# Second pass of the attention scores on 128 partition rows, the queries' low part written to both halves

## The chip, the cores and the metric

The kernel runs on one core of one Trainium2 chip. The metric is the device time of a run in microseconds; three runs of the kernel before have a median of 2206.68 us. Five engines work side by side, each through its own queue in order: TensorE (PE in the profile, its weight loads as PEld), VectorE (DVE), ScalarE (ACT), GpSimd (POOL) and SyncE (SP), which issues the DMAs.

## The reference, cut to what matters

One step of a layer for a prompt of 1024 tokens and a sample of 64 tokens with a cache of 1024. Four token mixers run over one projection of the input; the change is in mixer B, the forgetting attention with 8 heads of 64:

```python
def fox_attend(q, k, v, cq, ck, q_start):
    tq, tk = q.shape[1], k.shape[1]
    s = jnp.einsum('bqhd,bkhd->bhqk', q, k).astype(F32) * FX_HD ** -0.5
    s = s + jnp.swapaxes(cq, 1, 2)[..., :, None] - jnp.swapaxes(ck, 1, 2)[..., None, :]
    mask = jnp.arange(tk)[None, :] <= (q_start + jnp.arange(tq))[:, None]
    p = jax.nn.softmax(jnp.where(mask, s, NEG_BIG), axis=-1)
    return jnp.einsum('bhqk,bkhd->bqhd', p.astype(v.dtype), v)
```

The results of the four mixers are merged with gates, then follow an output projection with a norm, and a feed-forward part with a second norm.

## The kernel before

Everything is in f32, and the large matmuls are made of fp32r parts: a number is split into a high part (rounded to fp32r) and a low part (the rest, as fp32r), and `mm3` (lines 255 to 257) adds three matmuls for each 128 rows of the contraction: high by high, high by low, low by high. `dense` runs such a projection for 128 output columns of a weight, in three chunks of 384, 384 and 320 tokens. The mixers come in the order D, C, B, A. Within B the heads go in four pairs u = 0 to 3: the generator `P_B(u)` makes keys, queries and values of a pair with `dense`, and `M_B(u)` makes its attention. `branch` and `weave` emit `M_B(u-1)` side by side with `P_B(u)`, and the last `M_B(3)` beside the gates' dense work. So the attention's small matmuls lie between dense ones on TensorE. The framework's scheduler then sets each engine's order by its own estimates; buffers rotate in pools, and semaphores are put in by it.

`P_B` writes, for each head hh of a pair, a tile `kks[hh]` of 128 rows: the head's 64 rows r = 64 hh to 64 hh + 63 hold the keys' high part, the other 64 rows their low part (lines 927 and 928). `M_B` goes over 8 row blocks i of 128 queries. On every second i it makes, for 256 queries, a tile `q1` per head, with the queries' high part on both halves (GpSimd, line 1026), and one tile `ql` for both heads, each head's low part on its own 64 rows (VectorE, line 1027; q32 is the f32 query tile). For a head and row block the scores go into a two-bank PSUM tile `ps`, over Lw = max(128 (i + 1), 256) columns, in one block up to 512 columns and in two equal ones above. A block has two matmuls: a first pass (line 1038), whose 128 rows give high queries by high and by low keys at once, and a second pass (line 1040), low queries by high keys on the head's 64 rows. The last block of a row block adds the causal mask with a bf16 matmul of the identity (line 1043).

Then VectorE takes the scores with their bias and the smallest of them (line 1048), ScalarE the exponent with its sum (1053), VectorE the reciprocal and the scale (1054, 1055). One step later `second` transposes the weights `Pt` on TensorE (line 987) into PSUM, ScalarE and VectorE copy them to `PT` in turns (992, 994), and `third` multiplies with the values (line 1012, 64 output rows a head).

Of the kernel before, what the change touches and what calls it, by code (L numbers as in the profile page):

```python
# [9 lines left out]
F32 = mybir.dt.float32  # L10
F32R = mybir.dt.float32r
# [8 lines left out]
P = 128  # L20
D = 1024
# [47 lines left out]
def trunk_kernel(ctx: ExitStack, tc: tile.TileContext, I, O, dbg=None):  # L69
    nc = tc.nc  # L70
    PE, V, S, G, SP = nc.tensor, nc.vector, nc.scalar, nc.gpsimd, nc.sync
# [30 lines left out]
    def small(shape, s, bufs=3, dt=F32):  # L102
        return temps[1].tile(list(shape), dt, tag=s, name=nm(s), bufs=bufs)
# [4 lines left out]
    def const(shape, s, dt=F32):  # L108
        return cp.tile(list(shape), dt, tag=s, name=s)

    # ------------------------------------------------------------------ constants
    ident = const([P, P], "ident")
    make_identity(nc, ident)
    identb = const([P, P], "identb", BF16)
# [31 lines left out]
    mhalf = const([P, 1], "mhalf")  # L146
    V.memset(mhalf, -0.5)

    # ------------------------------------------------------------------ activations, transposed and split
    xh, xl = {}, {}  # L150

    def xtiles(s):
# [24 lines left out]
    def xsrc(tt):  # L177
        return I["x_prompt"][0, tt * P:(tt + 1) * P, :] if tt < 8 else I["x_sample"][0]

    # ------------------------------------------------------------------ weights: load, split, ring  # L180
    plan = []

    def win(c0):
# [73 lines left out]
            PE.matmul(ps, wl, mh, start=False, stop=i == n - 1)  # L257

    def mm2(ps, pairs):
        """as mm3, with both parts of 64 stationary columns side by side, to be added up by addup"""  # L260
        n = len(pairs)
        for i, (w, mh, ml) in enumerate(pairs):
            PE.matmul(ps, w, mh, start=i == 0, stop=False)
            PE.matmul(ps, w, ml, start=False, stop=i == n - 1)
# [20 lines left out]
            yield from g  # L285

    def weave(a, na, b, nb):
        """emit two streams side by side, na steps of a over nb steps of b"""
        live = [True, True]
        done = [0, 0]  # L290
        while live[0] or live[1]:
            i = 0 if live[0] and (not live[1] or done[0] * nb <= done[1] * na) else 1
            try:
                next((a, b)[i])
                done[i] += 1
            except StopIteration:
                live[i] = False

    # ------------------------------------------------------------------ start
    xtiles("x")  # L300
    pk = const([P, PK1], "pk")
    pkr = slot([P, P], F32, "pkr")
# [33 lines left out]
    n = PK1 - PK_NG  # L336
# [59 lines left out]
    oml = const([P, 4], "oml")  # L396
    V.tensor_scalar(oml, lb, -1.0, 1.0, OP.mult, OP.add)

    # ------------------------------------------------------------------ the sixteen gate columns, as rows
    zr_d = dp.tile([16, T], F32, name="zr_d")  # L400
    ls_d = dp.tile([16, T], F32, name="ls_d")
    cr_d = dp.tile([8, T], F32, name="cr_d")
# [122 lines left out]
            V.tensor_copy(mcol[0:TS, 8, 4 * j:4 * j + 4], p3[0:TS, 8, :])  # L525
            yield

    # ------------------------------------------------------------------ gated merge of one branch
    y_d = [[dp.tile([P, T], F32, name=f"y_d{m}_{j}") for j in range(3)] for m in range(4)]
    ylast = {}  # L530
    tails = []
# [67 lines left out]
        br(6)  # L599
        return res  # L600

    # ------------------------------------------------------------------ D: conv and RG-LRU
    SEG = ((0, TP, 3, 0), (TP, TS, TP + 6, TP + 3))
    wab = {}
    stD = const([P, 8, 4], "stD")
# [108 lines left out]
        SP.dma_start(O["p_rg_conv"][0, 0].rearrange("a (r p) -> (a r) p", p=P), so[8:20, :])  # L714
        SP.dma_start(O["s_rg_conv"][0, 0].rearrange("a (r p) -> (a r) p", p=P), so[20:32, :])

    # ------------------------------------------------------------------ C: HGRN2
    ams = []

    def blk(t, n=34):  # L720
# [31 lines left out]
    def M_C(u):  # L752
# [4 lines left out]
                V.memset(am, 0.0)  # L757
                ams.append(am)
        ou = oml[:, u:u + 1]
        # log of the forget gate: log sigmoid(z) + log(1 + lb exp(-z)), and sigmoid(-z)  # L760
        L = slot(s="L")
        S.activation(L, z, AF.Abs)
        S.activation(L, L, AF.Exp, scale=-1.0)
# [146 lines left out]
            yield  # L910
        tails.extend((lambda: tail(4, 8), lambda: tail(8, 9)))

    # ------------------------------------------------------------------ B: forgetting attention
    qbd = []

    def P_B(u):
        r0, r1 = slice(0, 64), slice(64, 128)
        k32 = slot(s="fk")
        bk = bc(FX_K + u * P)

        def evk(c, n0, n, ps):
            S.activation(k32[:, n0:n0 + n], ps, AF.Identity, bias=bk)
        yield from dense(("in", FX_K + u * P), evk)
        # each head's keys, both parts stacked on the partitions
        kks = [slot(dt=F32R, s="fkk") for _ in range(2)]
        for kk, r, q in zip(kks, (r0, r1), (r1, r0)):
            G.tensor_scalar(kk[r], k32[r], 1.0, 1.0, OP.mult, OP.mult)
            V.tensor_sub(kk[q], k32[r], kk[r].bitcast(F32))
        ks = small([P, TS], "fks", 2)
        G.tensor_copy(ks, k32[:, TP:T])  # L930
        q32 = slot(s="fq")

        def evq(c, n0, n, ps):
            S.activation(q32[:, n0:n0 + n], ps, AF.Identity, bias=bq8[:, u:u + 1], scale=0.125)
        dq = dense(("in", FX_Q + u * P), evq)
        next(dq)
        yield
        ko = slot([P, 9, P], s="fko")
        tok(ko, k32, "k", u)
        yield from dq  # L940
        vT = slot(s="fvT")
        bv = bc(FX_V + u * P)

        def evv(c, n0, n, ps):
            S.activation(vT[:, n0:n0 + n], ps, AF.Identity, bias=bv)
        yield from dense(("in", FX_V + u * P), evv)
        st["B", u] = kks, ks, q32, vT
# [2 lines left out]
        return ap.rearrange("t h d -> t (h d)")[:, u * P:(u + 1) * P]  # L950

    def tok(dst, src, nme, u):
        """keys or values with the tokens on the partitions, as they are returned"""
        for g0, g1 in ((0, 4), (4, 8), (8, 9)):
            w = tw(g0)
            pt = bank("m")
            p3 = pt.rearrange("p (a b) -> p a b", b=P)
            for tt in range(g0, g1):
                PE.transpose(p3[0:w, tt - g0, :], src[:, tt * P:tt * P + w], ident)
            if nme == "v":  # L960
                S.activation(dst[0:w, g0:g1, :], p3[0:w, 0:g1 - g0, :], AF.Copy)
            else:
                V.tensor_copy(dst[0:w, g0:g1, :], p3[0:w, 0:g1 - g0, :])
        SP.dma_start(flat(O["p_fox_" + nme][0, 0], u).rearrange("(t p) c -> p t c", p=P), dst[:, 0:8, :])
        SP.dma_start(flat(O["s_fox_" + nme][0, 0], u), dst[0:TS, 8, :])

    def M_B(u):
# [48 lines left out]
        for i in range(8):  # L1016
            L = (i + 1) * P
            if i % 2 == 0:
                t2 = slice(i * P, i * P + 2 * P)
                q1s = []  # L1020
                ql = small([P, 2 * P], "ql", 2, F32R)
                for hh in range(2):
                    r = slice(64 * hh, 64 * hh + 64)
                    q1 = small([P, 2 * P], f"q1{hh}", 2, F32R)
                    for h in (slice(0, 64), slice(64, 128)):
                        G.tensor_scalar(q1[h], q32[r, t2], 1.0, 1.0, OP.mult, OP.mult)
                    V.tensor_sub(ql[r], q32[r, t2], q1[r].bitcast(F32))
                    q1s.append(q1)
            qi = slice(i % 2 * P, i % 2 * P + P)
            for hh in range(2):  # L1030
                r = slice(64 * hh, 64 * hh + 64)
# [4 lines left out]
                for b in range(nb):  # L1036
                    s0, s1, o0 = b * n, b * n + n, 512 * b
                    PE.matmul(ps[:, o0:o0 + n], q1s[hh][:, qi], kks[hh][:, s0:s1], start=True, stop=False)  # L1038
                    last = s1 == Lw
                    PE.matmul(ps[:, o0:o0 + n], ql[r, qi], kks[hh][r, s0:s1], start=False, stop=not last)  # L1040
                    if last:
                        o = o0 + L - P - s0
                        PE.matmul(ps[:, o:o + P], identb, maskb, start=False, stop=True)
                # minus the scores with their bias, and minus the largest of them
                n = min(n, L)
                mn = small([P, 1], "mn", 4)
                Pt = slot([P, TP], s="Pt")
# [14 lines left out]
        second(*prev)  # L1062
        yield
        third()
        # decode rows: both heads on the partitions
        kr = slot([P, 8, P], s="fkr")
        SP.dma_start(kr, flat(I["cache_fox_k"][0, 0], u).rearrange("(t p) c -> p t c", p=P))
        vc = slot([P, 8, P], s="fvc")
# [45 lines left out]
        yput(1, u, y)  # L1114
        yield

    # ------------------------------------------------------------------ A: mLSTM
    def P_A(u):
        kt = slot(s="mkt")
        bk = bk8[:, u:u + 1]  # L1120
# [40 lines left out]
    def M_A(u):  # L1161
# [27 lines left out]
        yield  # L1189

        def first(c):
            """decays and scores of a block, and its keys with the tokens on the partitions"""
            w, t0 = tw(c), c * P
            pss, wes = [], []
            for hh in range(2):
# [100 lines left out]
            tails.extend((lambda hh=hh: tail(hh, 4, 8), lambda hh=hh: tail(hh, 8, 9)))  # L1296
        yield

    # ------------------------------------------------------------------ the token mixers
    def branch(m, Pg, Mg, n, nP, nM, it, ng=4):  # L1300
        for u in range(1, n):
            weave(Mg(u - 1), nM, Pg(u), nP)
# [24 lines left out]
    branch(0, P_A, M_A, 2, 18, 21, 3)  # L1327
    res = merge(0, 3)

    # ------------------------------------------------------------------ w_out, norm  # L1330
    phase("F")
    xtiles("mix")
    mxh, mxl = dict(xh), dict(xl)
# [72 lines left out]
                if i > 2:  # L1406
                    xsplit(acc[seq[i - 3]], seq[i - 3])

    # ------------------------------------------------------------------ gated conv feed-forward
    stF = const([P, 4, 16], "stF")  # L1410
    hs = {}

# [44 lines left out]
        SP.dma_start(O["y_prompt"][0, tt * P:tt * P + P, :] if tt < 8 else O["y_sample"][0], acc[tt][0:tw(tt)])  # L1457

    def stats(r, ps, al):
        """a tile's mean and its 1 / deviation, in halves"""  # L1460
        bst = small([P, 2, 6], "lst", 2)
        mv = small([P, 2], "lmv", 3)
        for hf, sl in enumerate(hfs):
            pinned(V.tensor_tensor(r[:, sl], r[:, sl], ps[:, sl], OP.add))
            pinned(V.bn_stats(bst[:, hf, :], r[:, sl]))
        pinned(V.bn_aggr(mv, bst))
        rs = small([P, 1], "lrs1", 2)
        pinned(V.tensor_scalar(rs, mv[:, 1:2], 1e-5, None, OP.add))
        G.tensor_tensor(rs, rs, mhalf, OP.pow)
        return mv, rs  # L1470

    def finish(s6, s7, gb, bb):
        """the last two tiles' norm, on the vector engine alone"""
        for tt, (mv, rs) in ((6, s6), (7, s7)):
            r = acc[tt]
            if tt == 7:
# [107 lines left out]
```

## Time and profile before

| | |
|---|---|
| runs, us | 2205.98, 2206.68, 2207.47 (median 2206.68) |
| profiled execution, span from first to last instruction | 2204.7 us |
| median of the runs less that span | 2.0 us |
| TensorE busy | 2161.4 us, 98% |
| VectorE / ScalarE / GpSimd busy | 1065.3 / 563.4 / 392.2 us |
| score matmuls, first to last start | 735.7 to 1043.5 us |
| TensorE clock granted | 1.00 in the stretch of the scores |

The profiled execution's own device time isn't listed apart from its span. In the profile a line such as L1040 is line 1040 of the kernel. A shape `64*128 64x320` means a stationary operand of 64 rows by 128 columns and a moving operand of 64 rows by 320 columns. Ends of matmuls are modelled, and matmuls overlap, so the distance from one start to the next says more than a duration.

### The profile page before, as it was taken

To read this page: it belongs to the slowest core of one execution; us is meant where nothing else is said; L and a number is where in the kernel's file an instruction comes from. 1 tells how busy PE (TensorE), PEld (TensorE's weight loads), DVE (VectorE), ACT (ScalarE), POOL (GpSimd) and SP (SyncE) were. 2 spreads that over 40 slices of the span, in tenths; PEclk is the share of its full clock that TensorE was granted. 3 is DMA by queue.
4 is the path that set the end of the run, shared out by engine and by line. 5 is a ranking of instruction groups with operands and counts; after the bars stand their busy time and mean duration, and the time that the engine had idled before them with its cause. 6 is when DMAs were issued, how large, how long until landed. Compare 5 with 4: busy or idle time off the path is not lost.

```text
span 2204.7 us, 31659 instructions
## 1 busy us (share of the span) xinstructions
PE 2161.4 (98%) x13203; PEld 1989.1 (90%) x13203; DVE 1065.3 (48%) x2020; ACT 563.4 (26%) x1100; POOL 392.2 (18%) x360
## 2 busy tenths in 40 slices
PE   8999999999999999999999999999999999999997
PEld 7999999888899887788999988997899999999996
DVE  4643346667334446445332144545564444444447
ACT  2753034454210333333201122221130011101111
POOL 1111001121123211111131102123320000000014
PEclk9999999999999999999999999999999999999999
DMA  5112321111133232130432112234101111111112
GB/s 148 52 59 89 100 63 39 43 52 44 63 132 127 67 91 78 51 88 26 136 130 78 59 31 82 73 119 159 48 20 43 34 58 39 48 48 39 48 57 83
DMA packets 174763, 156.76 MB, mean 71 GB/s; under 512 B 12637, under 2 KB 155305, under 8 KB 174621
## 3 DMA queue, kind: packets, MB, share of 16 engines
q1 hardware_dynamic: 174620, 154.74, 22.3%
q8 instruction: 104, 1.70, 0.3%
q14 instruction: 39, 0.31, 0.1%
HBM read 124.65 MB, written 30.06 MB: 70 GB/s over the span
## 4 chain that ended last, share of the span: by engine, by line
PE 85%; DVE 6%; issue 6%; POOL 1%; DMA 1%; ACT 0%; SPq 0%; DVEq 0%; POOLq 0%; ACTq 0%
PE psd L255 16%; PE psd L256 15%; PE psd L257 15%; PE psm L255 5%; PE psm L256 5%; PE psm L257 5%; PE pss L255 4%; PE pss L256 4%; PE pss L257 4%; PE psm L987 1%; DVE wl L244 1%; PE psm L1012 1%; PE pss L1040 1%; PE pss L1038 1%; POOL wh L243 1%
## 5 line engine op out<-in xcount | busy, mean ns | idle before, releaser
L255 PE MATMUL psd<-xh,wh 128*128 128x384 f32 (+1 forms) x1920 | 643.4, 335 | 1.0 <-ACT xh L164 0.9
L257 PE MATMUL psd<-xh,wl 128*128 128x384 f32 (+1 forms) x1920 | 631.8, 329 | 0.0
L256 PE MATMUL psd<-xl,wh 128*128 128x384 f32 (+1 forms) x1920 | 630.6, 328 | 0.5 <-DVE xl L165 0.5
L243 POOL TENSOR_SCALAR wh<-wr 128x1024 fp32r<-128x1024 f32 x144 | 155.0, 1078 | 1275.1 <-PE psd L256 436.9
L255 PEld LDWEIGHTS psd<-xh,wh 128*128 128x128 f32 x1920 | 363.2, 189 | 8.0 <-issue 3.0
L256 PEld LDWEIGHTS psd<-xl,wh 128*128 128x128 f32 x1920 | 362.0, 189 | 1.9 <-DVE xl L165 0.9
L257 PEld LDWEIGHTS psd<-xh,wl 128*128 128x128 f32 x1920 | 361.8, 188 | 0.5 <-DVE wl L244 0.2
L244 DVE TENSOR_TENSOR wl<-wr,wh 128x1024 fp32r<-128x1024 f32 x144 | 210.3, 1464 | 253.8 <-POOL wh L243 241.7
L552 ACT ACTIVATE th<-psd,bhalf 128x384 f32<-128x384 f32 (+1 forms) x96 | 53.9, 563 | 340.4 <-PE psd L257 339.7
L255 PE MATMUL psm<-yh,wh 128*128 128x384 f32 (+1 forms) x384 | 126.0, 330 | 7.7 <-DVE th L587 7.7
L255 PE MATMUL psd<-x1h,wh 128*128 128x384 f32 (+1 forms) x384 | 125.5, 327 | 0.7 <-DVE x1l L175 0.7
L255 PE MATMUL psm<-x1h,wh 128*128 128x384 f32 (+1 forms) x384 | 125.3, 326 | 0.7 <-DVE cv L1444 0.7
L256 PE MATMUL psm<-yl,wh 128*128 128x384 f32 (+1 forms) x384 | 125.5, 327 | 0.3 <-DVE yl L572 0.3
L257 PE MATMUL psm<-yh,wl 128*128 128x384 f32 (+1 forms) x384 | 125.7, 327 | 0.0
L257 PE MATMUL psd<-x1h,wl 128*128 128x384 f32 (+1 forms) x384 | 125.3, 326 | 0.0
L257 PE MATMUL psm<-x1h,wl 128*128 128x384 f32 (+1 forms) x384 | 125.2, 326 | 0.0
L256 PE MATMUL psd<-x1l,wh 128*128 128x384 f32 (+1 forms) x384 | 125.2, 326 | 0.0
L256 PE MATMUL psm<-x1l,wh 128*128 128x384 f32 (+1 forms) x384 | 125.2, 326 | 0.0
L587 DVE SCALAR_TENSOR_TENSOR th<-th,psm 128x384 f32<-128x384 f32 (+1 forms) x96 | 50.3, 529 | 107.6 <-PE psm L257 106.4
L1421 ACT ACTIVATE gp<-psd 128x384 f32<-128x384 f32 (+1 forms) x48 | 22.0, 457 | 302.3 <-PE psd L257 302.3
L1497 DVE SCALAR_TENSOR_TENSOR acc<-acc,pss 128x1024 f32<-128x1024 f32 x54 | 65.9, 1221 | 65.4 <-PE pss L257 64.7
L255 PE MATMUL pss<-wh,hh 128*128 128x512 f32 x208 | 83.0, 399 | 0.0
(479 smaller groups left out, 3570.0 us busy)
## 6 DMA issues: line engine op xcount, KB each, us to landing
wr<-in_w_in_dram SPq DMA_DIRECT2D x48, 512.0 KB
wr<-in_w_mg_dram SPq DMA_DIRECT2D x32, 512.0 KB
mx_d<-th SPq DMA_DIRECT2D x24, 544.0 KB
prev<-mx_d SPq DMA_DIRECT2D x24, 544.0 KB
wr<-in_w_br_dram SPq DMA_DIRECT2D x16, 512.0 KB
wr<-in_w_ff_gate_dram SPq DMA_DIRECT2D x16, 512.0 KB
wr<-in_w_ff_up_dram SPq DMA_DIRECT2D x16, 512.0 KB
wr<-in_w_ff_down_dram SPq DMA_DIRECT2D x16, 512.0 KB
```

The costliest lines, as they stand in the source:

```text
L243: G.tensor_scalar(h, raw, 1.0, 1.0, OP.mult, OP.mult)
L244: V.tensor_sub(l, raw, h.bitcast(F32))
L255: PE.matmul(ps, wh, mh, start=i == 0, stop=False)
L256: PE.matmul(ps, wh, ml, start=False, stop=False)
L257: PE.matmul(ps, wl, mh, start=False, stop=i == n - 1)
L552: S.activation(th[:, n0:n0 + n], ps, AF.Tanh, bias=b, scale=0.5)
L587: V.scalar_tensor_tensor(th[:, n0:n0 + n], th[:, n0:n0 + n], 1.0, ps[:, :n], OP.add, OP.mult)
L987: PE.transpose(p3[0:sw, j, 0:w], Pt[:, s0:s0 + sw], ident[0:w, 0:w])
L1012: PE.matmul(po[64 * h:64 * h + 64, 0:P], vt[:, j, 64 * h:64 * h + 64], pair[h][:, j, :], start=j == 0, stop=j == i)
L1038: PE.matmul(ps[:, o0:o0 + n], q1s[hh][:, qi], kks[hh][:, s0:s1], start=True, stop=False)
L1040: PE.matmul(ps[:, o0:o0 + n], ql[r, qi], kks[hh][r, s0:s1], start=False, stop=not last)
L1497: V.scalar_tensor_tensor(acc[tt], acc[tt], al, ps, OP.mult, OP.add)
```

## The change

`ql` is now one tile per head, `qls[hh]`, with the head's low query part on both halves, made by two subtractions in place of one. The second pass takes all 128 rows of `qls[hh]` and of `kks[hh]`; so it also adds the low queries by the low keys. The tiles ql0 and ql1 have two buffers each, as ql had. Comments are taken out elsewhere, and line numbers from 1028 on rise by one or two (1038 is now 1040, 1040 is 1042, 1043 is 1045, 1055 is 1057).

```diff
-                q1s = []
-                ql = small([P, 2 * P], "ql", 2, F32R)
+                q1s, qls = [], []
                 for hh in range(2):
                     r = slice(64 * hh, 64 * hh + 64)
                     q1 = small([P, 2 * P], f"q1{hh}", 2, F32R)
+                    ql = small([P, 2 * P], f"ql{hh}", 2, F32R)
                     for h in (slice(0, 64), slice(64, 128)):
                         G.tensor_scalar(q1[h], q32[r, t2], 1.0, 1.0, OP.mult, OP.mult)
-                    V.tensor_sub(ql[r], q32[r, t2], q1[r].bitcast(F32))
+                    for h in (slice(0, 64), slice(64, 128)):
+                        V.tensor_sub(ql[h], q32[r, t2], q1[r].bitcast(F32))
                     q1s.append(q1)
+                    qls.append(ql)
...
-                    PE.matmul(ps[:, o0:o0 + n], ql[r, qi], kks[hh][r, s0:s1], start=False, stop=not last)
+                    PE.matmul(ps[:, o0:o0 + n], qls[hh][:, qi], kks[hh][:, s0:s1], start=False, stop=not last)
```

TensorE, first pair of heads, end of row block i=1 and start of i=2, before (`fkk` is kks, `q` is q1, the numbers tell buffers apart):

```order
L1038 MATMUL pss_6722<-fkk_6395,q_911_6651 128x256
L1040 MATMUL pss_6722<-fkk_6395,ql_6646 128x256
L1043 LDWEIGHTS identb
L1043 MATMUL pss_6722<-maskb,identb 128x128
L1012 MATMUL psm_6733<-PT_6677,fvt_6594 64x128
L1038 MATMUL pss_6751<-fkk_6394,q_937_6743 128x384
L1040 MATMUL pss_6751<-fkk_6394,ql_6742 128x384
L1012 MATMUL psm_6733<-PT_6718,fvt_6594 64x128
```

The same place on TensorE after the change:

```order
L1040 MATMUL pss_6725<-fkk_6395,q_911_6652 128x256
L1042 MATMUL pss_6725<-fkk_6395,ql_912_6653 128x256
L1045 LDWEIGHTS identb
L1045 MATMUL pss_6725<-maskb,identb 128x128
L1012 MATMUL psm_6736<-PT_6680,fvt_6594 64x128
L1040 MATMUL pss_6757<-fkk_6394,q_937_6745 128x384
L1042 MATMUL pss_6757<-fkk_6394,ql_938_6746 128x384
L1012 MATMUL psm_6736<-PT_6721,fvt_6594 64x128
```

No score matmul has moved; the second pass now reads a ql of its own for each head. Elsewhere on TensorE some transposes (L987) stand one to six dense matmuls earlier or later.

VectorE at the softmax of row block i=1 of the first pair, before (`fq` is q32; sm, Pt and mn belong to the softmax):

```order
L1027 TENSOR_TENSOR ql_6900<-fq_6402,q_975_6901 64x256
L1054 RECIPROCAL sm_6714<-sm_6714 128x1
L1027 TENSOR_TENSOR ql_6900<-fq_6402,q_976_6905 64x256
L1055 TENSOR_SCALAR Pt_6712<-Pt_6712,sm_6714 128x256
L1054 RECIPROCAL sm_6729<-sm_6729 128x1
L1055 TENSOR_SCALAR Pt_6727<-Pt_6727,sm_6729 128x256
L1048 ISA Pt_6756,mn_6755<-pss_6751,fcb_6590 128x384
```

The same place on VectorE after the change:

```order
L1028 TENSOR_TENSOR ql_977_6907<-fq_6402,q_976_6906 64x256
L1056 RECIPROCAL sm_6717<-sm_6717 128x1
L1028 TENSOR_TENSOR ql_977_6907<-fq_6402,q_976_6906 64x256
L1057 TENSOR_SCALAR Pt_6715<-Pt_6715,sm_6717 128x256
L1056 RECIPROCAL sm_6732<-sm_6732 128x1
L1028 TENSOR_TENSOR ql_979_6913<-fq_6402,q_978_6912 64x256
L1057 TENSOR_SCALAR Pt_6730<-Pt_6730,sm_6732 128x256
L1050 ISA Pt_6762,mn_6761<-pss_6757,fcb_6590 128x384
```

The second head's first subtraction now stands between the reciprocal and the scale of the row block's second head, and its other one behind the next score row.

## Rows read from the trace of the kernel before

**Rows 1.** The page, its parts on busy time and on the chain.

```profile
PE 2161.4 (98%) x13203; PEld 1989.1 (90%) x13203; DVE 1065.3 (48%) x2020; ACT 563.4 (26%) x1100; POOL 392.2 (18%) x360
...
PE 85%; DVE 6%; issue 6%; POOL 1%; DMA 1%; ACT 0%; SPq 0%; DVEq 0%; POOLq 0%; ACTq 0%
```

**Rows 2.** Windows: busy PE, PEld, DVE, ACT, POOL; clock; DMA share; GB/s.

```profile
735.00:1070.00 335.00, 333.46 (x2346) 270.08 (x2345) 167.79 (x394) 123.90 (x283) 52.56 (x84) 1.00 0.24 68
```

**Rows 3.** Waits of PE, 735 to 1070 us: total, times, longest.

```profile
PE psm L987 <- DVE Pt L1055: 1.5, 3, 0.5
```

**Rows 4.** Waits of PEld in the same stretch.

```profile
PEld pss L1040 <- issue: 19.0, 89, 0.3
PEld L1043 <- issue: 9.4, 46, 0.2
PEld pss L1038 <- issue: 7.4, 38, 0.2
```

**Rows 5.** Line 1040: count, min/median/max ns, starts, four commonest forms.

```profile
L1040 PE MATMUL pss<-fkk,ql x96: 379/440/503, 736.1 to 1043.5; 64*128 64x384 f32 x24, 64*128 64x512 f32 x24, 64*128 64x256 f32 x16, 64*128 64x320 f32 x16
```

**Rows 6.** Timeline of PE, ends of two full-array runs: start, duration, engine, line.

```profile
746.50 0.31 PE L257 MATMUL psd<-xh,wl 128*128 128x320 f32 x1
...
748.41 0.34 PE L1038 MATMUL pss<-fkk,q 128*128 128x384 f32 x1
...
2149.67 0.39 PE L257 MATMUL pss<-wh,hl 128*128 128x512 f32 x1
...
2152.92 0.39 PE L256 MATMUL pss<-wd,hh 128*128 128x512 f32 x1
```

**Rows 7.** Timeline of PE at a narrow score row and at a wide one.

```profile
735.89 0.28 PE L1038 MATMUL pss<-fkk,q 128*128 128x256 f32 x1
736.10 0.39 PE L1040 MATMUL pss<-fkk,ql 64*128 64x256 f32 x1
736.42 0.23 PE L1043 MATMUL pss<-maskb,identb 128*128 128x128 bf16 x1
...
841.13 0.41 PE L1038 MATMUL pss<-fkk,q 128*128 128x320 f32 x1
841.48 0.41 PE L1040 MATMUL pss<-fkk,ql 64*128 64x320 f32 x1
841.82 0.23 PE L1043 MATMUL pss<-maskb,identb 128*128 128x128 bf16 x1
841.86 0.39 PE L1038 MATMUL pss<-fkk,q 128*128 128x320 f32 x1
```

**Rows 8.** Chain in order of time: start, length; 384, 448, 448 and 512 columns.

```profile
771.60 0.37 PE pss L1040
...
778.83 0.40 PE pss L1040
779.23 0.40 PE pss L1038
...
784.71 0.43 PE pss L1040
```

**Rows 9.** Timeline: a dense matmul, the load beside it, and a second pass's load.

```profile
735.02 0.33 PE L256 MATMUL psd<-xl,wh 128*128 128x384 f32 x1
...
735.02 0.19 PEld L257 LDWEIGHTS psd<-xh,wl 128*128 128x128 f32 x1
...
736.10 0.18 PEld L1040 LDWEIGHTS pss<-fkk,ql 64*128 64x128 f32 x1 [0.19 <-issue]
```

**Rows 10.** VectorE's ql group (busy, mean ns | idle before); timeline of scales and transposes.

```profile
L1027 DVE TENSOR_TENSOR ql<-fq,q 64x256 fp32r<-64x256 f32 x32 | 14.5, 452 | 18.6 <-PE pss L1040 13.5 <-POOL q L1026 4.6
...
745.43 0.35 DVE L1055 TENSOR_SCALAR Pt<-Pt,sm 128x256 f32<-128x256 f32 x1
746.13 0.38 PE L987 MATMUL psm<-ident,Pt 128*128 128x128 f32 x2
...
751.81 1.33 DVE L1055 TENSOR_SCALAR Pt<-Pt,sm 128x384 f32<-128x384 f32 x1
```

## The prediction

> **What bounds the kernel now.** I read the page first: TensorE is busy for 2161 of 2204.7 us and holds 85% of the chain that ended last [rows 1]. The change touches the stage of the forgetting attention only, so I then read the stretch in which its score matmuls lie, 735 to 1070 us. There TensorE is busy for 333.5 of 335 us, VectorE for 167.8 and ScalarE for 123.9, at full granted clock [rows 2], and the whole list of TensorE's waits is three waits of 0.5 us each [rows 3]. A microsecond taken off TensorE in this stretch comes off the end, unless another engine cannot follow.
>
> Busy is not the same as streaming, though. The weight loads (PEld) show where it isn't: before the load of the second pass (L1040) the loader stands idle 89 times, 19.0 us in all, before the mask's load (L1043) 46 times and before that of the first pass (L1038) 38 times, and all of these are put down to issue, not to another engine [rows 4]. The reader is to see the pattern of shapes: L1040 has the form `64*128` while L1038 and L1043 have `128*128` [rows 5, 7].
>
> What it costs is seen from start to start. Matmuls of `128*128` that follow each other start at the pace of their columns: 13 of 320 columns take 748.41 - 746.50 = 1.91 us, 0.147 each, and 14 of 512 columns take 2152.92 - 2149.67 = 3.25 us, 0.232 each [rows 6]. That is 0.456 ns a column on average, so I take 0.117 us for 256 columns, 0.175 for 384 and 0.204 for 448. Around the second pass the pace is another one [rows 7]: with 320 columns, L1038 to L1040 takes 0.35 us, L1040 to L1043 0.34. With 256 columns L1040 takes 0.32 and L1038, which there follows full-array work, 0.21. The chain gives the other widths as pieces of L1040: 0.37 for 384 columns, 0.40 for 448 and 0.43 for 512, and 0.40 for an L1038 of 448 that follows an L1040 [rows 8]. So L1040 takes 0.19 to 0.20 us more than its columns at every width: a constant, not a rate. An L1038 between two second passes has the same excess, and one that comes from full-array work and goes into L1040 has half, 0.21 - 0.117 = 0.093. I read this as follows: each change of array shape lets the matmul ahead run out (about 0.10 us) and then leaves the next load uncovered (about 0.10 us).
>
> **The change part by part.**
>
> *Second pass at 128 rows.* With qls on both halves, L1040 has the shape of its neighbours, and both changes of shape around it go. L1040 occurs 96 times [rows 5]; the kernel's loops give 16 of 256 columns, 16 of 320, 24 of 384, 16 of 448 and 24 of 512. Its excess: 16 x (0.32 - 0.117) = 3.2; 16 x (0.34 - 0.147) = 3.1; 24 x (0.37 - 0.175) = 4.7; 16 x (0.40 - 0.204) = 3.1; 24 x (0.43 - 0.232) = 4.8. Sum 18.9 us. Of the 96, three are followed by the `128*64` matmuls of L1012, which keep their own change of shape, so 0.3 is left: 18.6 us.
>
> *First pass.* 32 of the 96 L1038 open the second block of a wide score row and lie between two second passes. They lose the whole excess, 0.20 each: 6.4 us. The other 64 lose only the running out, about 0.095: 6.1 us. Their uncovered load, where they follow L1012 or a short transpose, stays. Together the sum on TensorE is 18.6 + 6.4 + 6.1 = 31.1 us. None of this is cover for something else, because TensorE sets the pace of the stretch.
>
> *256 columns.* The trace has no run of full-array matmuls that narrow. Their load has 128 columns like the others, and the nearest row shows loads of this size keeping a pace of 0.147 [rows 6]. If that is their floor, 32 matmuls cost up to 0.03 more than I took, 1.0 us; I take 0.5.
>
> *The mask.* L1043 is bf16 and follows L1040 nearly always. That a bf16 load behind a 128-row f32 matmul costs no running out is not shown. The other direction is: L1043 to L1038 takes 0.04 us [rows 7]. So I take 0 and keep 61 x 0.10 = 6.1 us as the far end. On the other side the mask's own load, idle for 0.2 us 46 times [rows 4], may come to lie under the second pass: half of that idle is the running out counted above, the other half, 46 x 0.1 = 4.6 us, mostly runs beside the next load, which stays uncovered behind so short a matmul. I take none of it and keep 3 us as an end of the range.
>
> *Products added.* The second pass now also adds low query times low key. It streams the same columns, and the pace of a 128-row matmul is that of rows 6, so nothing more.
>
> *VectorE.* Each ql subtraction is made twice: 32 more of 64x256, 0.452 us each, 14.5 us by the group's row [rows 10]. The order shows most of them doubled in place, where VectorE waits anyway (167 us are free in the stretch [rows 2]); so most cost nothing. One place is tight: a new subtraction stands between the reciprocal and the scale of score row i=1, hh=1. The scale there starts at 745.43 and takes 0.35, and the transposes that wait for it start at 746.13 [rows 10], a slack of 0.35. With 0.42 to 0.45 more and TensorE arriving some 0.2 earlier there, a wait of about 0.25 comes up, four times (once a head pair): 1.0 us. The far ends are 0 and, if a quarter of the 32 subtractions were exposed in full, 3.6 us. The three present waits stay as they are: the wait at L987 hangs on a score row's end, through VectorE, and moves with it. SBUF tiles, GpSimd's q1 copies and all DMA issues are unchanged in number and order, so they cost nothing. ScalarE, with 124 of 335 us, follows.
>
> The sum: 31.1 - 0.5 - 1.0 = 29.6 us. The profiled execution has a span of 2204.7 us, 2.0 below the median of the runs, and I carry that difference over: 2206.7 - 29.6 = 2177 us.
>
> **A rule that speaks against it.** The trace shows the load of one 128-row matmul running beside the matmul before it, with the same rows in use: the load for L257 and the matmul of L256 both start at 735.02, while the load for L1040 starts only with an idle 0.19 us before it [rows 9]. The Trainium skill, "TensorE: Matmul & The Clock Gate", Part 3, "The mechanism", lists as seen in traces that weight loads overlap matmuls in flight only when the row group differs. By that sentence a full-height second pass would cover no more than the half-height one and the sum would be zero, rival 2 below; row 735.02 disagrees, and the sum above goes by the row.
>
> **The rivals.**
>
> 1. *The mask keeps its run-out* (a change of type costs as a change of shape does). For: L1043's loads are idle 46 times [rows 4]. Against: 0.04 us in the other direction. Gain 29.6 - 6.1 = 23.5, 2183 us.
>
> 2. *The change doesn't do what it says*: the stall belongs to the pair of operands q and ql or to the accumulation in one bank, and a full-height second pass stalls too. For: every stall lies at this pair. Against: the dense matmuls switch operands and accumulate at full pace. Gain about 0, less the 1.0 on VectorE: 2206 to 2208 us.
>
> 3. *VectorE becomes the one that is waited for.* A large part of the 32 subtractions lands between a score row and its transposes: half of them exposed in full are 7.2 us, gain 30.6 - 7.2 = 23, 2183 us; all of them 14.5, 2191 us.
>
> 4. *Slower.* The same place, but the subtractions come under the slowing that the scale shows at 751.81, where 128x384 takes 1.33 us [rows 10]: each of 32 then holds TensorE for 1.33 us, 42.6 us against 30.6 gained, 2219 us. It decides from 30.6 / 32 = 0.96 us on the path per subtraction. The subtractions of now have a mean of 0.452 [rows 10], with the same neighbours on GpSimd, so nearly all of them would have to be slowed and exposed at once: unlikely.
>
> **How the numbers follow.** The forecast, 2177 us, has a chance of 0.78 with its own bounds: 31.1 (nothing lost) gives 2175.6 and the 3 us at the mask 2172.6; the upper end, 3.6 on VectorE and 1.0 at 256 columns, gives 2180. Rival 1 has 0.07, rival 3 0.07, rival 2 0.04, rival 4 0.04. For 8 in 10 the range goes from 2172.5 to 2186, which takes in rival 1 and the half of rival 3. About 0.2% (4.4 us) is what a measurement of this kernel can tell from no change. Faster by more than that: 0.78 + 0.07 + 0.07 = 0.92; within it 0.04; slower 0.04.
>
> **What would show it.** The second pass reads `128*128` and its pieces of the chain shrink to the pace of rows 6, from 0.34 to about 0.15 at 320 columns; the idle before its loads, 19.0 us, goes nearly to zero, and that before the first pass's from 7.4 to the few behind L1012 and the transposes. TensorE's waits in the stretch grow from 1.5 us to 2 to 5, on the scale. VectorE's ql group counts 64 and about 29 us. The rest of the trace shifts by 30 us and keeps its lengths. It would be wrong if the second pass at `128*128` kept a pace above 0.2 us at 320 columns, or if waits for VectorE of tens of microseconds stood in the list.

## The result and the profile after

The changed kernel takes 2183.14 us (median of 4 runs, 2182.15 to 2185.64); its ratio to the kernel before is 0.9894, 95% interval 0.988 to 0.9908. That is 23.5 us less. The prediction of 2177 us had the way right and the time 6 us too low; 2183 lies inside its range. The profiled execution is the longest of the four, with a span of 2183.9 us.

Tables first. The page's busy times and chain, the stretch from the first to the last score matmul (columns as in [rows 2]) and the waits of TensorE in it (as in [rows 3]). Lines from 1028 on have moved: the first pass is L1040 now, the second L1042, the mask L1045, VectorE's score row L1050 and its scale L1057.

```profile
PE 2133.7 (98%) x13203; PEld 1986.1 (91%) x13203; DVE 1079.4 (49%) x2052; ACT 563.4 (26%) x1100; POOL 396.1 (18%) x360
...
PE 82%; DVE 8%; issue 6%; POOL 2%; DMA 1%; ACT 1%; SPq 0%; DVEq 0%; POOLq 0%; ACTq 0%
```

```profile
736.00:1021.00 285.00, 278.91 (x2123) 243.48 (x2121) 169.81 (x404) 115.98 (x265) 54.75 (x83) 1.00 0.24 69
```

```profile
PE pss L1040 <- DVE mn L1050: 3.6, 3, 1.2
PE psm L987 <- DVE Pt L1057: 2.5, 7, 0.4
```

The score stage is about 24 us shorter, and in it VectorE now has two places where TensorE waits for it: 3.6 us at a first pass, which was not there, and 2.5 us at the transposes, where there were 1.5 [rows 3]. All ten of these waits are new; the three of before are gone.

The stalls of shape are gone. The second pass as its line's view shows it (count, min/median/max ns, first and last start, forms), and the waits of PEld in the stage, to be read against [rows 4, 5]:

```profile
L1042 PE MATMUL pss<-fkk,ql x96: 278/338/481, 736.8 to 1020.6; 128*128 128x384 f32 x24, 128*128 128x512 f32 x24, 128*128 128x256 f32 x16, 128*128 128x320 f32 x16
```

```profile
PEld L1045 <- issue: 8.2, 38, 0.3
PEld pss L1040 <- POOL q L1026: 3.9, 3, 1.3
...
PEld pss L1040 <- issue: 1.0, 6, 0.2
```

L1042 has no idle at all before its loads, where there were 19.0 us. On the timeline of PE (start, duration) the narrow row and the first wide rows of the first pair read:

```profile
736.66 0.28 PE L1040 MATMUL pss<-fkk,q 128*128 128x256 f32 x1
736.78 0.28 PE L1042 MATMUL pss<-fkk,ql 128*128 128x256 f32 x1
736.90 0.23 PE L1045 MATMUL pss<-maskb,identb 128*128 128x128 bf16 x1
...
756.75 0.31 PE L1042 MATMUL pss<-fkk,ql 128*128 128x320 f32 x1
756.90 0.31 PE L1040 MATMUL pss<-fkk,q 128*128 128x320 f32 x1
757.05 0.31 PE L1042 MATMUL pss<-fkk,ql 128*128 128x320 f32 x1
757.20 0.23 PE L1045 MATMUL pss<-maskb,identb 128*128 128x128 bf16 x1
758.63 0.39 PE L1040 MATMUL pss<-fkk,q 128*128 128x320 f32 x1 [1.20 <-DVE mn L1050]
```

At 256 columns both passes take 0.12 us from start to start, at 320 columns 0.15: the pace of the columns. The last two rows show what came instead: from the mask at 757.20 to the next first pass at 758.63 there are 1.43 us, where a mask used to be followed after 0.04 [rows 7].

Added up over all starts of the stage, first and second pass together took 68.3 us before and take 38.0 now, 30.3 less: 12.2 at the first pass and 18.1 at the second. From the first to the last score matmul the stage went from 307.6 to 284.0 us, 23.6 less. The difference of 6.7 lies in the masks with what follows them (5.3 us before, 9.6 now, nearly all of it the three gaps of 1.43) and in dense matmuls with a wait behind them (152.4 and 154.5).

### Where VectorE came in

The timelines of DVE and POOL of the changed kernel at the end of row block i=2 and the start of i=3, first pair; a pair's later twin stands 76 us further on, and the third 153:

```profile
751.11 0.41 DVE L1057 TENSOR_SCALAR Pt<-Pt,sm 128x384 f32<-128x384 f32 x1
751.44 2.54 DVE L1028 TENSOR_TENSOR ql<-fq,q 64x256 fp32r<-64x256 f32 x2
754.01 0.16 DVE L1056 RECIPROCAL sm<-sm 128x1 f32<-128x1 f32 x1
...
755.06 2.69 DVE L928 TENSOR_TENSOR fkk<-fk,fkk 64x1088 fp32r<-64x1088 f32 x2
757.78 0.69 DVE L1050 CUSTOM_DVE_ANT_0 Pt<-pss,fcb 128x512 f32<-128x512 f32 x1
758.40 0.08 DVE L1050 DVE_READ_ACCUMULATOR2_ANT mn<- 128x1 f32 x1
758.51 0.86 DVE L1028 TENSOR_TENSOR ql<-fq,q 64x256 fp32r<-64x256 f32 x2
```

```profile
751.34 2.37 POOL L927 TENSOR_SCALAR fkk<-fk 64x1088 fp32r<-64x1088 f32 x2
755.16 2.87 POOL L1026 TENSOR_SCALAR q<-fq 64x256 fp32r<-64x256 f32 x2 [1.44 <-PE pss L1040]
```

Two subtractions take 0.86 us at 758.51, and 2.54 us at 751.44, beside GpSimd's two copies of the next pair's keys (L927). The queue behind them is late by that: the keys' low part (L928) and then the score row i=3, hh=1, whose matmuls had ended by 755.4 and which VectorE takes only at 757.78. That row holds one of the two PSUM tiles (the memory that the score matmuls write to), and the first pass of i=4, hh=1 waits for it. Before the change VectorE took the same row at nearly the same time, 757.66, but there the row's mask, its last matmul, had started only at 757.03 (timelines of DVE and of PE of the kernel before):

```profile
755.02 2.60 DVE L928 TENSOR_TENSOR fkk<-fk,fkk 64x1088 fp32r<-64x1088 f32 x2
757.66 0.69 DVE L1048 CUSTOM_DVE_ANT_0 Pt<-pss,fcb 128x512 f32<-128x512 f32 x1
...
757.03 0.23 PE L1043 MATMUL pss<-maskb,identb 128*128 128x128 bf16 x1
```

So at this place TensorE's saving ran into a VectorE queue that had not become shorter. Before the change the copies of L927 had stood beside the scale at 751.81 [rows 10], which took 1.33 us; now the scale is through in 0.41 us and the subtractions stand there.

VectorE is not the only one that is late at this first pass. Its load also waits for GpSimd's q1 copies (3.9 us in three, in PEld's list above). Two of these copies take 2.87 us at 755.16, beside VectorE's L928, and end at 758.03; two others had taken 1.23 at 750.02. VectorE lets the PSUM tile go last, at 758.48, and so ends the wait; but with VectorE on time, about 0.8 of each gap of 1.43 us would have stood, by an estimate from these rows.

Three of the seven waits at the transposes (1.0 us) follow 2.35 us behind these first passes, for the scale of the row that VectorE took late. The other four (1.4 us), one for each head pair, lie elsewhere, at row block i=6. VectorE and TensorE in the first pair:

```profile
781.78 0.95 DVE L1028 TENSOR_TENSOR ql<-fq,q 64x256 fp32r<-64x256 f32 x2 [0.38 <-POOL q L1026]
...
782.84 1.21 DVE L1050 CUSTOM_DVE_ANT_0 Pt<-pss,fcb 128x1024 f32<-128x1024 f32 x1
...
783.97 0.68 DVE L1057 TENSOR_SCALAR Pt<-Pt,sm 128x896 f32<-128x896 f32 x1
...
784.80 0.63 PE L987 MATMUL psm<-ident,Pt 128*128 128x128 f32 x4 [0.39 <-DVE Pt L1057]
```

Two subtractions stand here ahead of the next score row and of the scale that the transposes need.

### The profile page after: what moved, and what is told of

The parts are those of the page before. It is cut to its first block, busy times and chain, and to the rows that moved or that the text cites. A ratio compares the mean times of both kernels' runs of the same rounds, so it can differ in the third digit from the quotient of the medians.

```text
span 2183.9 us, 31686 instructions
## 1 busy us (share of the span) xinstructions
PE 2133.7 (98%) x13203; PEld 1986.1 (91%) x13203; DVE 1079.4 (49%) x2052; ACT 563.4 (26%) x1100; POOL 396.1 (18%) x360
## 4 chain that ended last, share of the span: by engine, by line
PE 82%; DVE 8%; issue 6%; POOL 2%; DMA 1%; ACT 1%; SPq 0%; DVEq 0%; POOLq 0%; ACTq 0%
PE psd L255 15%; PE psd L257 15%; PE psd L256 15%; PE psm L255 5%; PE psm L256 5%; PE psm L257 5%; PE pss L255 4%; PE pss L256 4%; PE pss L257 4%; DVE wl L244 2%; PE psm L987 1%; PE psm L1012 1%; POOL wh L243 1%; DVE ql L1028 1%; PE psm L1200 1%
## 5 line engine op out<-in xcount | busy, mean ns | idle before, releaser
L244 DVE TENSOR_TENSOR wl<-wr,wh 128x1024 fp32r<-128x1024 f32 x144 | 210.5, 1465 | 253.5 <-POOL wh L243 239.6
L1432 DVE TENSOR_SCALAR cv<-gp,pk 128x1024 f32<-128x1024 f32 (+1 forms) x32 | 21.1, 698 | 126.9 <-ACT gp L1423 126.9
```

Source lines behind the costliest of these rows:

```text
L244: V.tensor_sub(l, raw, h.bitcast(F32))
```

## The experiments

Six kernels; each ratio below is to runs of the kernel before on the same chip.

### The zero half: shape without the added subtractions

```diff
-                    ql = small([P, 2 * P], f"ql{hh}", 2, F32R)
+                    ql = qz[hh][i // 2 % 2]
...
-                    for h in (slice(0, 64), slice(64, 128)):
-                        V.tensor_sub(ql[h], q32[r, t2], q1[r].bitcast(F32))
+                    V.tensor_sub(ql[r], q32[r, t2], q1[r].bitcast(F32))
```

`qz` holds two tiles per head whose other half is set to zero once, at the start of the stage.

> The second pass keeps its 128 rows, but the half of each ql tile that belongs to the other keys part is zero, written once at the start; each ql subtraction is made once, as in the kernel before (32 in all). Shape theory (the whole gain on TensorE comes from the change of shape, and what is missing of it was eaten by the 32 added VectorE subtractions): TensorE's score matmuls keep the starts of the changed kernel, the waits of L1040 for VectorE and GpSimd (3.6 us) and most of those of the transposes are gone, and the time is 2206.6 - 30 = 2176 to 2179 us, 4 to 7 us below the changed kernel. Rival (the missing part has another cause, such as later stages or the mask): the time stays at 2182 to 2184 us.

2178.15 us, ratio 0.9871 (0.9856 to 0.9886): 28.9 us off, 5 more than the change. Its line of the second pass and its only wait of TensorE in the stage:

```profile
L1047 PE MATMUL pss<-fkk,qz x96: 274/338/481, 735.0 to 1013.1; 128*128 128x384 f32 x24, 128*128 128x512 f32 x24, 128*128 128x256 f32 x16, 128*128 128x320 f32 x16
```

```profile
PE pss L1045 <- DVE mn L1055: 0.5, 3, 0.2
```

From first to last second pass the stage takes 278.1 us, against 283.8 with the change and 307.4 before [rows 5]. The two passes together are at 38.0 us, as in the changed kernel. So the shape alone gives the 30 us on TensorE, and the added subtractions took back 5 to 6. As expected. The rival, that later stages or the mask ate the rest, falls: neither was touched. Three subtractions, one at each of the three places, still run beside the copies of the keys, and 0.39 to 0.45 us are left of each gap of 1.43.

### The subtractions alone

```diff
-                    PE.matmul(ps[:, o0:o0 + n], qls[hh][:, qi], kks[hh][:, s0:s1], start=False, stop=not last)
+                    PE.matmul(ps[:, o0:o0 + n], qls[hh][r, qi], kks[hh][r, s0:s1], start=False, stop=not last)
```

> The changed kernel with the second pass put back on the head's own 64 rows; the 32 added subtractions stay. Shape theory: the stalls around the second pass are all back, and with TensorE as slow as before most of the added VectorE work is hidden: 2206 to 2210 us. Rival (the gain came with the new tiles or the new order of the instructions, not with the shape): clearly below 2200 us.

2209.43 us, ratio 1.0008 (1.0 to 1.0017). The waits of PEld are those of [rows 4] again, and TensorE's list those of [rows 3]:

```profile
PEld pss L1042 <- issue: 19.0, 89, 0.3
PEld L1045 <- issue: 9.4, 46, 0.2
PEld pss L1040 <- issue: 7.4, 38, 0.2
```

```profile
PE psm L987 <- DVE Pt L1057: 1.5, 3, 0.5
```

With the second pass at half height, 32 more subtractions cost next to nothing (0.08%, and the interval reaches down to no change). Three of them run beside the copies of L927 here, for up to 1310 ns each (six do in the changed kernel), and TensorE is late enough for VectorE all the same. So the gain came with the shape and not with new tiles or a new order, and the price of the subtractions depends on how fast TensorE is.

### The keys' high part on ScalarE

```diff
-            G.tensor_scalar(kk[r], k32[r], 1.0, 1.0, OP.mult, OP.mult)
+            S.activation(kk[r], k32[r], AF.Copy)
```

> The changed kernel with the keys' high part (line 927) written by ScalarE in place of GpSimd; all 64 subtractions stay. In the changed kernel two subtractions at 751.4 us take 2.54 us beside two GpSimd copies of line 927, against 0.86 elsewhere, and the score row i=4, hh=1 waits 1.2 us three times after it. Theory of contention between VectorE and GpSimd: without line 927 on GpSimd the two take 0.86 again, the three waits go, and the time is 4 to 6 us below the changed kernel, 2177 to 2179 us. Rival (the number of subtractions in the queue is what delays the chain, whoever else runs): the waits stay at 1 us or move, and the time stays within 1.5 us of 2183 us.

2176.41 us, ratio 0.9863 (0.985 to 0.9877). The waits at the first pass are gone, and the same two subtractions on DVE's timeline take a third:

```profile
746.25 0.41 DVE L1057 TENSOR_SCALAR Pt<-Pt,sm 128x384 f32<-128x384 f32 x1
746.58 0.84 DVE L1028 TENSOR_TENSOR ql<-fq,q 64x256 fp32r<-64x256 f32 x2
```

```profile
PE psm L987 <- DVE Pt L1057: 1.4, 4, 0.4
```

All 64 subtractions are there, so their number does not make the wait at the first pass; what stands beside GpSimd's copies does. The edit frees GpSimd's own queue along with VectorE's, so it does not part the two. The four waits that are left are those at i=6: they are the price of added subtractions away from the copies. The time fell a little more than expected.

The second passes start at 731.9 instead of 736.8 us. Most of that is no effect of the edit. VectorE's timelines ahead of the stage, of the changed kernel and then of this one:

```profile
705.98 2.10 DVE L244 TENSOR_TENSOR wl<-wr,wh 128x1024 fp32r<-128x1024 f32 x1 [8.28 <-POOL wh L243]
708.12 3.38 DVE L928 TENSOR_TENSOR fkk<-fk,fkk 64x1088 fp32r<-64x1088 f32 x2
```

```profile
702.74 1.23 DVE L244 TENSOR_TENSOR wl<-wr,wh 128x1024 fp32r<-128x1024 f32 x1 [8.29 <-POOL wh L243]
704.00 2.60 DVE L928 TENSOR_TENSOR fkk<-fk,fkk 64x1088 fp32r<-64x1088 f32 x2
```

L244 stands ahead of the first pair's keys and starts 3.2 us sooner. That difference between the two profiled executions is there near their start already: TensorE's first matmul of L426 stands at 44.6 and at 41.5 us. The keys' low part ends 4.9 us sooner, at 706.60 against 711.50, so the edit brings the start forward by 1.7. The next experiment prices this.

### The same move on the kernel before

Line 927 as above, nothing else changed.

> The kernel before, with nothing but the keys' high part moved from GpSimd to ScalarE: what that move is worth without the change. Theory: the first score row starts some 4 us earlier, the three waits of 0.5 us in the stage go, and the stage is otherwise as long as before: 2201 to 2204 us. If the move is worth as much here as it was on the changed kernel (6 to 7 us), 2200 us, then it repaired nothing that the change had broken.

2204.28 us, ratio 0.9984 (0.9975 to 0.9993), 3.5 us off; 0.3 above the upper end of what was expected. Its second pass:

```profile
L1040 PE MATMUL pss<-fkk,ql x96: 379/440/502, 733.6 to 1038.9; 64*128 64x384 f32 x24, 64*128 64x512 f32 x24, 64*128 64x256 f32 x16, 64*128 64x320 f32 x16
```

From the first to the last second pass the stage takes 305.3 us, 2.1 less than before. On the changed kernel the move was worth 6.7 us in the runs (2183.14 to 2176.41) and 5.2 in the stage (283.8 to 278.6). So about 3 us, in the runs and in the stage alike, are the contention that the change had run into, and the rest would have come without it.

### Both repairs together

> Both repairs together: the zero half (32 subtractions, each made once) and the keys' high part on ScalarE. Theory (the shape gives 30 us, contention at line 927 had eaten some 6 of them, and line 927 off GpSimd also brings the first score row some 4 us forward): the stage from the first to the last second pass has the length of the zero-half run, 278 us, the start is that of the run with the keys on ScalarE, 732 us, and the time is 2173 to 2176 us. Rival (both repairs and the early start are worth the same thing): 2176 to 2178 us, no lower than the keys on ScalarE alone.

The edits are the two shown above. 2174.76 us, ratio 0.9852 (0.9838 to 0.9865): 33.0 us off, the lowest median here, faster than both the kernel before and the changed one.

```profile
L1047 PE MATMUL pss<-fkk,qz x96: 278/338/472, 733.5 to 1010.4; 128*128 128x384 f32 x24, 128*128 128x512 f32 x24, 128*128 128x256 f32 x16, 128*128 128x320 f32 x16
```

The stage takes 276.9 us and has no wait of TensorE left in it. It starts at 733.5, not at the 732 expected, which had counted in a difference between profiled executions that the keys' move does not make. Against the keys' move alone it gains 1.7 us in the stage's length; in the runs' times the two intervals overlap, so that step alone isn't secured.

### Grouped passes: half height kept, fewer changes of shape

On the kernel before:

```diff
                     PE.matmul(ps[:, o0:o0 + n], q1s[hh][:, qi], kks[hh][:, s0:s1], start=True, stop=False)
+                for b in range(nb):
+                    s0, s1, o0 = b * n, b * n + n, 512 * b
                     last = s1 == Lw
```

> The kernel before with 64-row second passes, but in the 32 wide score rows both first passes come ahead of both second passes: 1, 1, 2, 2 in place of 1, 2, 1, 2. So two changes of array shape of four go in each wide row, and nothing else. Shape theory (a change costs 0.20 us, run-out and uncovered load): 32 x 2 x 0.20 = 12.8 us less, 2194 us, if a 64-row load overlaps the 64-row matmul ahead of it. Rival (a half-height pass costs its 0.2 us by itself, whatever stands ahead): 2206 us, no change.

2197.1 us, ratio 0.9956 (0.9944 to 0.9969): 10 us off, with every second pass still on 64 rows. PE's timeline at a row of 448 columns, and PEld's rows of the same matmuls:

```profile
777.54 0.56 PE L1038 MATMUL pss<-fkk,q 128*128 128x448 f32 x2
778.03 0.68 PE L1042 MATMUL pss<-fkk,ql 64*128 64x448 f32 x2
778.64 0.23 PE L1045 MATMUL pss<-maskb,identb 128*128 128x128 bf16 x1
```

```profile
778.03 0.29 PEld L1042 LDWEIGHTS pss<-fkk,ql 64*128 64x128 f32 x2 [0.30 <-issue]
778.63 0.10 PEld L1045 LDWEIGHTS <-identb 128*128 128x128 bf16 x1 [0.31 <-issue]
```

Two second passes take 0.61 us from start to start, so the pair pays its excess once: 0.61 - 2 x 0.204 = 0.20. One load stands uncovered for the pair, not two. Over the whole stage the starts of both passes, 96 matmuls each, come to 56.2 us, 12.2 below the kernel before, against 12.8 expected; of these the stage's length kept 11.3 and the runs' times 10. A half-height pass costs nothing extra by itself. The change of shape does.

## Why the prediction was right or wrong, point by point

**Right: what bounds the stage, and the price of a change of shape.** The sum on TensorE was 31.1 less 0.5 for 256 columns, 30.6; measured from the starts it was 30.3, and its parts fit too: 18.1 at the second pass for 18.6, and 12.2 at the first for 12.5. The two widths read above are at 0.12 and 0.15 us. At 256 columns the load puts no floor under it: 0.12 is the 0.117 of the columns, so even the 0.5 was not needed.

**Right: no run-out at the mask.** L1042 to L1045 takes 0.12 us at 256 columns and L1045 to the next pass 0.04: a bf16 matmul behind an fp32r one costs no change of shape. Rival 1, which gave the measured time almost to the microsecond (2183), is wrong in its mechanism. That PEld still shows 8.2 us of issue before the mask's load costs nothing that the starts would show.

**Right: rows against the rule.** The Trainium skill's sentence in "TensorE: Matmul & The Clock Gate", Part 3, "The mechanism", that loads overlap only where the row group differs, would have left the time at 2206. The changed kernel has the first and the second pass on the same 128 rows, each load covered; in the grouped kernel the second of two half-height loads is covered on the same 64 rows.

**Wrong: the term of VectorE.** It stood in the sum with 1.0 us, four waits of 0.25 at the scale of i=1, hh=1, and with 3.6 as the far end. It measured 6.7: 30.3 off the matmuls, 23.6 off the stage. So 2183 lies above the forecast's own upper end, 2180, and is inside the range only because the range took in rivals 1 and 3. The place was wrong too. At i=1 the scale came at 745.39 and its transposes did not wait. Four waits at a scale, one for each head pair, did come, but at i=6, 1.4 us in all. The larger part came at i=3 and i=4, through the PSUM tile of a score row that VectorE took late, and at the transposes behind it.

Two things had been left out of the step. First, a subtraction was priced at its mean, 0.452 us, wherever it was moved. But in the changed order two of them stand ahead of the reciprocal of i=3, in the stretch where GpSimd copies the next keys, and the row of the scale at 751.81 showed what that stretch does: 1.33 us in place of 0.41. That row was used for rival 4 only, where all 32 had to be slowed to turn the sign. It should have priced the two at this place, 2.54 us for a pair, three times. The experiment on ScalarE confirms the neighbour: the same pair takes 0.84 there. The Trainium skill, "SBUF — State Buffer", "Who interferes with whom", says that a VectorE instruction with two SBUF inputs contends with a GpSimd instruction that reads SBUF. The traces agree, 2.54 us beside the copies and 0.84 without them. Second, the free time of VectorE, 167 us in the stage, was taken as cover. Free time elsewhere doesn't help a queue that is late at one place.

**Rival 3** was thus the right one in kind: VectorE is waited for. That its half of the subtractions exposed in full gives 2183 too is luck: in fact few were exposed, and most of their price is that of the slowed ones. **Rival 4**, slower, had the right contention and far too many places for it. **Rival 2** falls with the pace of the second pass, 0.15 us at 320 columns, and with the subtractions alone: with the old shape nothing is gained.

**Signs named beforehand.** The idle before the second pass's loads went to zero, and that before the first pass's from 7.4 to 1.0 us of issue, as said. TensorE's waits in the stage were to be 2 to 5 us, at the scale; they are 6.1, and 3.6 of them at the first pass. The ql group counts 64, with 33.3 us in place of 29:

```profile
L1028 DVE TENSOR_TENSOR ql<-fq,q 64x256 fp32r<-64x256 f32 x64 | 33.3, 520 | 5.5 <-POOL q L1026 4.4
```

The mean of 520 ns against 452 [rows 10] was the first thing to look at.

**Open.** Of the 6.7 us that the stage kept back, 3.1 hang on the copies of line 927 (5.2 less 2.1, by the move with the change and without it). Another 1.8 (1.7 by the rounded starts above) go with the added subtractions when the keys' copies don't slow them, by the stage of the keys on ScalarE against that of both repairs; the runs' intervals overlap there, so only the traces show it. The last 1.8 are kept back with both repairs too: from the first to the last score matmul that kernel's stage is 28.6 us shorter than that of the kernel before with the same move, not 30.3, though its list has no wait of TensorE left. What holds them was not tested. Of the profiled execution's 20.8 us, another 3 us were lost outside the stage. The 0.8 before its first score row stand in VectorE's L244 ahead of the first keys already (705.21 before the change, 705.98 after), so the change did not make them. Behind the stage's last score row the profile of before has 1161.2 us, that of the changed kernel 1163.3, and the experiments have 1161.6 to 1163.2, with 1162.7 and 1163.2 for grouped passes and for the subtractions alone, which keep the old shape. These 2.1 us do not follow the shape. One of them is a longer wait of the merge's first matmuls for ScalarE and VectorE (1.3 us against 0.3); the cause is open.

## What to carry to other kernels

Look for matmuls of another array shape between full ones, in starts, not in durations: each visit here cost 0.3 to 0.4 us for going in and coming out, whatever its width (30.3 us for 96 visits, 12.2 for the 32 that grouping saved), so a short half-height pass among full ones is worth padding with zeros to full height, or at least putting next to its like. Pad with zeros that are written once rather than with a second copy that must be made every time. And when a bound engine gets faster, price what the change adds to the next engine at the places where that engine is already late or slowed, not by its mean and its idle share.

## What the runs showed of the hardware

A change between 128 and 64 rows cost about 0.20 us between two f32 score passes at every width from 256 to 512 columns, read from the starts as 0.10 of run-out and 0.10 of uncovered load; a change between fp32r and bf16 at the same shape cost nothing that the starts show (0.12 us at 256 columns, 0.04 behind the mask). Full-array fp32r matmuls of 256 columns held 0.12 us from start to start, although their loads are drawn 0.19 us long. Two VectorE subtractions of 64x256 took 0.84 to 0.86 us alone and 2.54 us beside two GpSimd copies of 64x1088; two GpSimd copies of 64x256 took 1.23 us at 750.02 and 2.87 us beside two VectorE subtractions of 64x1088.
